# Seven products for eight in part of a SwiGLU FFN: two block pairs per layer by quadrants

## The chip, the cores and the metric

The kernel runs on one core of a Trainium2 chip. The metric is the device time of one execution in microseconds. TensorE (PE in the profile) multiplies matrices, VectorE (DVE) and ScalarE (ACT) do elementwise work, GpSimd (POOL) does small work for the norms, and SyncE (SP) issues the DMAs.

## The reference

Two layers of a hybrid encoder run over 256 tokens with a model width of 1024, in fp32. The part that is changed is the first half of the SwiGLU FFN and, by its place, the per-layer embedding:

```python
h = h + rms_norm(mixed @ w_out, g_mix_post)

gate, up = jnp.split(rms_norm(h, g_ffn_pre) @ w_ffn_in, 2, axis=-1)   # 1024 -> 2 * 2816
h = h + rms_norm((jax.nn.silu(gate) * up) @ w_ffn_out, g_ffn_post)

e = p_i @ w_ple_proj                                                  # 256 -> 1024
h = h + rms_norm(jax.nn.sigmoid(h @ w_ple_gate) * e, g_ple_post)
```

Ahead of it stand one projection of the normed state, two attention branches (gated linear attention and grouped-query attention) and their merge.

## The kernel before

**Numbers.** Every fp32 operand is split into a high part (a cast to the matmul's fp32r type, on ScalarE) and a low part (source minus high, on VectorE); this is `split`, lines 99 to 102, with the subtraction in `vsub` (line 97). A product takes three matmuls into one accumulator: high with high, high with low, low with high (`mm3`, line 87, recorded at line 85).

**Weights.** All weights pass through one `Stream` (line 177) in the order of the list `plan` (line 162). A unit is 128 partitions by 2048 fp32 values, 1 MB: four k-blocks of 128 rows by 512 columns. It is loaded by SyncE into one of two `raw` tiles, split in two halves of 1024 into one of four pairs of tiles `wh` and `wl`, and then used. `Stream.done` is called after the last matmul on a unit; it lets the next unit of the plan be split (`fill`), and once a raw tile has been split the next load is issued. At most `depth` units, four, are held split at a time.

**Tiles.** Tokens are worked in two halves of 128. `amode` (line 383) multiplies one half of the tokens (stationary, 128x128) by one unit (moving, 512 columns): 12 matmuls. `project` (line 417) does two units for both halves: 48 matmuls. Activations that are to be multiplied are transposed by TensorE and split into a `Split` (line 258), which has one large tile for the high parts and one for the low ones.

**Order around the change.** A `Task` is a piece of work that is put off: it waits for a number of ticks, and `tick` is called once for every six matmuls of a 128x512 product. So transposes are laid between matmuls of later work. `need` forces a task that is wanted at once. The framework puts every engine's instructions in an order of its own by priority, with all waits; `tc.high_priority` moves some ahead.

Per layer, the parts near the change run in this order:
- `wout`: `by_half` (line 426) first works the output projection for token half 0, then for half 1. After each half come `post_norm_add` and `pre_norm`, whose transposes into `u2` wait six ticks (`WAIT`).
- `emb`: the embedding's product, 24 matmuls on one unit, none of them with a tick. Its copies from the accumulators run on ScalarE (line 1023).
- `ffnin`: eleven blocks. A block is 256 gate columns and the same 256 up columns, so its two units hold gate and up side by side. For blocks 0 and 1 token half 0 goes first (48 matmuls), then half 1; blocks 2 to 10 go through `project`. Each block ends with a silu on ScalarE (lines 1038 and 1051) and a multiplication on VectorE (line 94); its transposes wait four ticks (`WAIT_FFN`).
- `ffnout`: eleven units of `w_ffn_out`, of which the last four are worked for half 0 first and then for half 1; then `post_norm_add` and the transposes of `h` into `hT`, five ticks later (`WAIT_H`).
- `ple`: the embedding's gate, by halves, with the embedding `e` as a factor.

The pools hold 2 `raw`, 4 `wh`, 4 `wl`, 9 `big` (2048 columns), 10 `mid` (1024), 5 `t512` and 8 accumulators (128x512).

Of the kernel before, what the change touches and what calls it, by code (L numbers as in the profile page):

```python
# [2 lines left out]

# [27 lines left out]
HIDDEN = 2816  # L31
NBLK = HIDDEN // 256
UNIT = 2112
RQ = ((0, 288), (288, 672), (672, 1056))
# [5 lines left out]
def trunk_kernel(ctx: ExitStack, tc: tile.TileContext, a: dict, out: bass.AP):  # L40
# [122 lines left out]
    for l in range(DEPTH):  # L163
        w = a["w_in"][l]
        plan += [unit_rows(w, n, C_RA, C_RA + 1056, 2 if l + n == 0 else 1) for n in range(4)]
        for c0 in (C_AK, C_GQ, C_GK, C_GV, C_GV + 512, C_GG, C_GG + 512, C_GA, C_GA + 512, C_GB, C_GB + 512):
            plan += [unit(w, kh, c0) for kh in range(2)]
        for j in range(2):
            for wo in (a["w_o_gla"][l], a["w_o_attn"][l]):
                plan += [unit(wo, kh, j * 512) for kh in range(2)]  # L170
        plan += [unit(a["w_out"][l], kh, j * 512) for kh in range(2) for j in range(2)]
        plan += [unit_rows(a["w_ple_proj"][l], 0)]
        plan += [unit_gate_up(a["w_ffn_in"][l], kh, b) for b in range(NBLK) for kh in range(2)]
        plan += [unit_rows(a["w_ffn_out"][l], n) for n in range(NBLK)]
        plan += [unit(a["w_ple_gate"][l], kh, j * 512) for kh in range(2) for j in range(2)]

    class Stream:


        def __init__(self, depth):  # L180
            self.depth, self.n, self.held, self.raws, self.ready, self.open = depth, 0, 0, [], [], False

        def load(self, between=lambda: None):

            if self.n == len(plan):
                return
            raw = rawp.tile([P, UNIT], F32, tag="raw", name=nm("raw"))
            moves = plan[self.n](raw)
            for dst, src in moves:
                if self.open:  # L190
                    nc.sync.dma_start(dst, src)
                else:
                    on("dma", nc.sync.dma_start, dst, src)
                between()
            self.raws.append((raw, sum(math.prod(dst.shape[1:]) for dst, _ in moves)))
            self.n += 1

        def pieces(self):

            raw, n = self.raws.pop(0)  # L200
# [4 lines left out]
            return [(wh[:, c], wl[:, c], raw[:, c]) for c in (slice(0, n // 2), slice(n // 2, n))]  # L205

        def fill(self):
            while self.open and self.held < self.depth and self.raws:
                for piece in self.pieces():
                    split(*piece)  # L210
                self.load()

# [4 lines left out]
        def done(self, n=1):  # L217
            self.held -= n
            self.fill()

# [37 lines left out]
    class Split:  # L258


        def __init__(self):
            self.h, self.l = (big(F32R).rearrange("p (k t) -> p k t", t=T) for _ in range(2))
            self.makers = {0: [], 1: []}

        def need(self, hf, k=None):
# [9 lines left out]
        def put(self, src, k, n, t0, tn):  # L275

            i = (slice(None), slice(k, k + n), slice(t0, t0 + tn))
            split(self.h[i], self.l[i], src.rearrange("p (k t) -> p k t", t=tn))

        def tok(self, k, hf):  # L280
            s = slice(hf * P, (hf + 1) * P)
            return self.h[:, k, s], self.l[:, k, s]

        def all(self, k):
            return self.h[:, k, :], self.l[:, k, :]

    def transpose_in(sp, src, k, n, hf):

        ps = aux()
        for i in range(n):  # L290
            nc.tensor.transpose(ps[:, i * P : (i + 1) * P], src[:, i * P : (i + 1) * P], ident)
        with tc.high_priority(AHEAD):
            sp.put(ps[:, : n * P], k, n, hf * P, P)

    last_pow = [None]
# [47 lines left out]

    def turn_in(sp, x, hf, wait):


        def turn():
            yield wait
            for j, y in enumerate(halves(x)):
                transpose_in(sp, y, 4 * j, 4, hf)  # L350

        sp.makers[hf].append(Task(turn(), part[0]))

    def pre_norm(g, hf, sp, wait=WAIT):

# [6 lines left out]

        turn_in(sp, xn, hf, wait)

# [27 lines left out]
    def wmode(os_, sp, k0, w, first, last):  # L392
# [9 lines left out]
        for f in range(4):  # L402
            o = os_[f // 2][:, (f % 2) * T : (f % 2 + 1) * T]
            s = slice(f * P, (f + 1) * P)
            for k in range(4):
# [3 lines left out]
                )  # L409
            tick()  # L410

    def project_t(sp):
# [113 lines left out]
    def turned(hf, k, n):  # L526

        ps = aux()
        for i in range(n):
            on("pe", nc.tensor.transpose, ps[:, i * P : (i + 1) * P], xn[hf][:, (k + i) * P : (k + i + 1) * P], ident)  # L530
        i = (slice(None), slice(k, k + n), slice(hf * P, (hf + 1) * P))
        split_here(uT.h[i], uT.l[i], ps[:, : n * P].rearrange("p (k t) -> p k t", t=P))

# [42 lines left out]
    for l in range(DEPTH):  # L576
# [413 lines left out]

        part[0] = f"{l}emb"
        e = big().rearrange("p (s c) -> p s c", s=2)
        pin = t512().rearrange("p (s c) -> p s c", c=256)
        nc.sync.dma_start(pin, a["p"][l, 0].rearrange("(s p) c -> p s c", p=P))
        pT = [t.rearrange("p (k t) -> p k t", t=T) for t in halves(mid(F32R))]
        ps = aux()
        for k in range(2):
            for hf in range(2):
                nc.tensor.transpose(
                    ps[:, k * T + hf * P : k * T + (hf + 1) * P], pin[:, hf, k * P : (k + 1) * P], ident  # L1000
                )
        split(pT[0], pT[1], ps.rearrange("p (k t) -> p k t", t=T))
# [4 lines left out]
        u2 = Split()  # L1007

        def after_out(hf, o):
            post_norm_add(o, gpost, hf)  # L1010
            pre_norm(gpre, hf, u2)

        by_half(mixT, after_out)

        part[0] = f"{l}emb"
        wh, wl = (t[:, :2048].rearrange("p (k c) -> p k c", c=512) for t in ws.take())
        for hf in range(2):
            s = slice(hf * P, (hf + 1) * P)
            for j in range(2):
                o = acc()  # L1020
                for k in range(2):
                    mm3(o, (pT[0][:, k, s], pT[1][:, k, s]), (wh[:, 2 * k + j, :], wl[:, 2 * k + j, :]), k == 0, k == 1)
                nc.scalar.copy(e[:, hf, j * 512 : (j + 1) * 512], o)
        ws.done()


        part[0] = f"{l}ffnin"
        hid = [Split() for _ in range(3)]
        us = [[ws.take() for _ in range(2)] for _ in range(2)]
        for hf in range(2):  # L1030
            for b in range(2):
                o = acc()
# [5 lines left out]
                nc.scalar.activation(sg[:, 0:256], o[:, 0:256], AF.Silu)  # L1038
                vmul(sg[:, 0:256], o[:, 256:512], sg[:, 0:256])


                def turn(sg=sg, b=b, hf=hf):
                    yield WAIT_FFN
                    transpose_in(hid[0], sg[:, 0:256], b * 2, 2, hf)

                hid[0].makers[hf].append(Task(turn(), part[0]))
        for b in range(2, NBLK):
            sg = t512()
            for hf, o in enumerate(project(u2)):
                c = slice(hf * 256, (hf + 1) * 256)  # L1050
                nc.scalar.activation(sg[:, c], o[:, 0:256], AF.Silu)
                vmul(sg[:, c], o[:, 256:512], sg[:, c])

            def turn(sg=sg, b=b):
                yield WAIT_FFN
                ps = aux()
                for k in range(2):
                    for hf in range(2):
                        nc.tensor.transpose(
                            ps[:, k * T + hf * P : k * T + (hf + 1) * P],  # L1060
                            sg[:, hf * 256 + k * P : hf * 256 + (k + 1) * P], ident,
                        )
                with tc.high_priority(AHEAD):
                    hid[b // 4].put(ps, 2 * b % 8, 2, 0, T)

            turned = Task(turn(), part[0], 2 * b % 8 // 4)
            for hf in range(2):
                hid[b // 4].makers[hf].append(turned)

        if l + 1 < DEPTH:  # L1070
            ropes = rope_tables(l + 1)
            wup_next = up_weights(l + 1)


# [5 lines left out]
        def out_step(n, hf, w):  # L1080
            wh, wl = (t[:, :2048].rearrange("p (k c) -> p k c", c=512) for t in w)
            for kk in range(2):
                k = 2 * n + kk
                hid[k // 8].need(hf, k % 8)
                for j in range(2):
                    mm3(
                        o[hf][j], hid[k // 8].tok(k % 8, hf), (wh[:, 2 * kk + j, :], wl[:, 2 * kk + j, :]),
                        k == 0, k == 2 * NBLK - 1,
# [10 lines left out]
        for hf in range(2):  # L1099
# [5 lines left out]

            turn_in(hT, h[:, hf, :], hf, WAIT_H)


# [77 lines left out]
```

## Time and profile before

| | us |
|---|---|
| median of 3 runs | 950.26 (949.28 to 950.45) |
| the profiled execution's own time | 950.44 |
| its span | 948.7 |
| TensorE busy in the span | 936.2 |
| VectorE busy | 612.8 |
| ScalarE busy | 509.9 |
| FFN-in of layer 0, start to end | 266.55 to 391.93 |

The profile is one execution with a record of every instruction. The page gives busy times, the chain of work that ended last and groups of instructions by line; the trace can also be asked for the time line of one engine, for the waits between engines, and for the busy time in any stretch. Matmul records overlap, because matmuls are pipelined: what one costs is seen from how far apart a run of them starts and ends. Where several instructions follow each other on an engine, the timeline merges them into one row with a count (x2).

### The profile page before, as it was taken

The numbers are of one execution on the slowest core, as the hardware profiler recorded it, in microseconds if no ns is written. First come the engines' busy times: TensorE is split into PE (matmuls) and PEld (weight loads), VectorE is DVE, ScalarE is ACT, GpSimd is POOL, SyncE is SP. The second block draws the span as 40 slices with busy tenths as digits, with TensorE's granted clock in tenths as the row PEclk, the third lists the DMA queues.
The fourth block names the chain that finished last, engine by engine and source line by source line (L and its number), as shares of the span: only waits on it lengthen the run. The fifth ranks groups of instructions, "written<-read, shape, count | busy, mean of one in ns | idle before, by whom it ended". The sixth has DMA issues, their size and how long they took to land.

```text
span 948.7 us, 12370 instructions
## 1 busy us (share of the span) xinstructions
PE 936.2 (99%) x4769; PEld 798.5 (84%) x4769; DVE 612.8 (65%) x838; ACT 509.9 (54%) x872; POOL 83.3 (9%) x152
## 2 busy tenths in 40 slices
PE   8999999999999999999999999999999999999996
PEld 7998888888888888888889988888888888888886
DVE  4798977456666555444779799663667665555364
ACT  4669776434465544443666686754436554443343
POOL 3400211000020000000133011200001000000010
PEclk9999999999999999999999999999999999999999
DMA  6463454655478655553545525355564666655531
GB/s 237 156 222 133 147 176 142 219 180 185 146 225 271 216 178 178 180 211 121 190 169 178 192 75 189 107 204 199 200 222 134 221 223 192 192 192 178 183 128 44
DMA packets 100760, 169.25 MB, mean 178 GB/s; under 512 B 3735, under 2 KB 51351, under 8 KB 100702
## 3 DMA queue, kind: packets, MB, share of 16 engines
q1 hardware_dynamic: 100702, 168.47, 52.7%
q8 instruction: 37, 0.61, 0.2%
q14 instruction: 21, 0.17, 0.0%
HBM read 167.41 MB, written 1.05 MB: 178 GB/s over the span
## 4 chain that ended last, share of the span: by engine, by line
PE 94%; DVE 2%; POOL 1%; ACT 1%; DMA 1%; issue 1%; SPq 0%; POOLq 0%; DVEq 0%; ACTq 0%
PE acc_0ffnin L85 13%; PE acc_1ffnin L85 13%; PE acc_0ffnout L85 6%; PE acc_1ffnout L85 6%; PE acc_0gate L85 5%; PE acc_1gate L85 5%; PE acc_1merge L85 5%; PE acc_0merge L85 5%; PE acc_1gqk L85 2%; PE acc_0rq L85 2%; PE acc_0gqk L85 2%; PE acc_1wout L85 2%; PE acc_0wout L85 2%; PE acc_1ple L85 2%; PE acc_1gg L85 2%; PE acc_0gg L85 2%
## 5 line engine op out<-in xcount | busy, mean ns | idle before, releaser
L85 PE MATMUL acc_0ffnin<-wh_0ffnin,big_0wout 128*128 128x512 f32 x288 | 91.3, 393 | 0.0
L85 PE MATMUL acc_1ffnin<-wh_1ffnin,big_1wout 128*128 128x512 f32 x288 | 91.3, 393 | 0.0
L97 DVE TENSOR_TENSOR wl_1ffnin<-raw_1ffnin,wh_1ffnin 128x1024 fp32r<-128x1024 f32 x40 | 47.9, 1221 | 48.4 <-ACT wh_1ffnin L101 48.4
L97 DVE TENSOR_TENSOR wl_0ffnin<-raw_0ffnin,wh_0ffnin 128x1024 fp32r<-128x1024 f32 x40 | 47.8, 1222 | 43.3 <-ACT wh_0ffnin L101 43.2
L101 ACT CAST wh_1ffnin<-raw_1ffnin 128x1024 fp32r<-128x1024 f32 x40 | 41.1, 1053 | 51.0 <-PE acc_1ffnin L85 38.2
L101 ACT CAST wh_0ffnin<-raw_0ffnin 128x1024 fp32r<-128x1024 f32 x40 | 40.8, 1052 | 44.7 <-PE acc_0ffnin L85 35.3
L85 PEld LDWEIGHTS acc_0ffnin<-wh_0ffnin,big_0wout 128*128 128x128 f32 x288 | 54.1, 188 | 11.0
L85 PEld LDWEIGHTS acc_1ffnin<-wh_1ffnin,big_1wout 128*128 128x128 f32 x288 | 54.1, 188 | 11.0
L85 PE MATMUL acc_1ffnin<-wl_1ffnin,big_1wout 128*128 128x512 f32 x144 | 56.1, 390 | 0.0
L85 PE MATMUL acc_0ffnin<-wl_0ffnin,big_0wout 128*128 128x512 f32 x144 | 56.1, 390 | 0.0
L85 PE MATMUL acc_0ffnout<-wh_0ffnout,big_0ffnin 128*128 128x512 f32 x112 | 34.9, 390 | 0.0
L85 PE MATMUL acc_1ffnout<-wh_1ffnout,big_1ffnin 128*128 128x512 f32 x112 | 34.9, 390 | 0.0
L97 DVE TENSOR_TENSOR wl_1ffnout<-raw_1ffnout,wh_1ffnout 128x1024 fp32r<-128x1024 f32 x18 | 21.3, 1222 | 18.4 <-ACT wh_1ffnout L101 18.4
L97 DVE TENSOR_TENSOR wl_0ffnout<-raw_0ffnout,wh_0ffnout 128x1024 fp32r<-128x1024 f32 x18 | 21.3, 1222 | 18.4 <-ACT wh_0ffnout L101 18.4
L85 PEld LDWEIGHTS acc_1ffnin<-wl_1ffnin,big_1wout 128*128 128x128 f32 x144 | 27.1, 188 | 5.3
L85 PEld LDWEIGHTS acc_0ffnin<-wl_0ffnin,big_0wout 128*128 128x128 f32 x144 | 27.1, 188 | 5.3
L101 ACT CAST wh_1ffnout<-raw_1ffnout 128x1024 fp32r<-128x1024 f32 x18 | 18.1, 1052 | 22.6 <-PE acc_1ffnout L85 22.6
L101 ACT CAST wh_0ffnout<-raw_0ffnout 128x1024 fp32r<-128x1024 f32 x18 | 18.2, 1053 | 22.5 <-PE acc_0ffnout L85 19.8
L97 DVE TENSOR_TENSOR wl_1gate<-raw_1gate,wh_1gate 128x1024 fp32r<-128x1024 f32 x14 | 16.5, 1222 | 17.8 <-ACT wh_1gate L101 17.8
L97 DVE TENSOR_TENSOR wl_0gate<-raw_0gate,wh_0gate 128x1024 fp32r<-128x1024 f32 x14 | 16.5, 1222 | 17.8 <-ACT wh_0gate L101 17.8
L85 PE MATMUL acc_0rq<-wh_start,big_start 128*128 128x384 f32 (+1 forms) x96 | 25.4, 349 | 0.9 <-ACT big_start L111 0.9
L85 PE MATMUL acc_0gate<-wh_0gate,big_start 128*128 128x512 f32 x80 | 24.8, 389 | 0.0
(587 smaller groups left out, 2672.7 us busy)
## 6 DMA issues: line engine op xcount, KB each, us to landing
raw_0ffnin<-in_w_ffn_in_dram SPq DMA_DIRECT2D x32, 512.0 KB, 4.2
raw_1ffnin<-in_w_ffn_in_dram SPq DMA_DIRECT2D x32, 512.0 KB, 3.9
raw_0ffnin<-in_w_ffn_out_dram SPq DMA_DIRECT2D x6, 1024.0 KB, 5.0
raw_1ffnin<-in_w_ffn_out_dram SPq DMA_DIRECT2D x6, 1024.0 KB, 4.9
raw_0ffnout<-in_w_ffn_out_dram SPq DMA_DIRECT2D x5, 1024.0 KB, 4.9
raw_1ffnout<-in_w_ffn_out_dram SPq DMA_DIRECT2D x5, 1024.0 KB, 4.9
raw_0rq<-in_w_in_dram SPq DMA_DIRECT2D x4, 1024.0 KB, 5.0
raw_0v<-in_w_in_dram SPq DMA_DIRECT2D x4, 1024.0 KB, 4.8
```

What stands on the lines that cost most here:

```text
L85: return nc.tensor.matmul(o, lhsT, rhs, start=start, stop=stop)
L97: nc.vector.tensor_tensor(out=out, in0=in0, in1=in1, op=ALU.subtract)
L101: nc.scalar.copy(hi, src)
```

## The change

Blocks 2 and 3, and blocks 6 and 7, are worked as pairs. A pair is a product of the 256x1024 normed activations with 1024x1024 weights (512 gate columns and 512 up columns). Both are cut into quadrants: token half by half of the 1024 rows, and half of the rows by gate or up. The four quadrant results are made from seven products of 12 matmuls with sums of quadrants (the scheme of Winograd) in place of eight. The four activation sums are made once per layer on VectorE, from fp32 copies of the transposed activations (`plain`, copied by ScalarE), and split (`sums`). The weight sums are made on VectorE for each pair, in place, in the tiles that the raw quadrants were loaded into (`Stream.step`): two quadrants are loaded into a `wh` and a `wl` tile that the stream lends, which counts as one held unit; one goes into a `big` tile and one into a `raw` tile. After each of the first, second, third and fifth splits an addition of 128x2048 prepares a later one. The results of the products are combined by copies on ScalarE and additions on VectorE (`seven`), and two accumulators stay open over much of the pair.

`FFN_IN` gives the order after blocks 0 and 1: u is one unit of a plain block (both token halves, 24 matmuls), a digit is that product of a pair. The plain blocks are 4, 5, 8, 9 and 10. The transposes of a pair's hidden columns wait nine ticks.

The embedding moves: its load of `p`, the transposes and the split stand behind FFN-in, its weights' unit is loaded behind `w_ffn_out`, and its product stands between `ffnout` and `ple`. `Split` now has one tile for four k-blocks, with high and low parts side by side, taken when first written.

```diff
+FFN_IN = "uu12u34u5u67uu12u34u5u67"
+WAIT_PAIR = 9
+PLAIN, PAIRS = (4, 5, 8, 9, 10), (2, 6)
...
-        plan += [unit_rows(a["w_ple_proj"][l], 0)]
-        plan += [unit_gate_up(a["w_ffn_in"][l], kh, b) for b in range(NBLK) for kh in range(2)]
-        plan += [unit_rows(a["w_ffn_out"][l], n) for n in range(NBLK)]
+        w = a["w_ffn_in"][l]
+        blocks = [[unit_gate_up(w, kh, b) for kh in range(2)] for b in range(NBLK)]
+        plan += blocks[0] + blocks[1]
+        plains = [u for b in PLAIN for u in blocks[b]]
+        pairs = [[unit(w, kh, c + b * 256) for kh in range(2) for c in (0, HIDDEN)] for b in PAIRS]
+        for x in FFN_IN:
+            if x == "1":
+                pair = pairs.pop(0)
+            plan.append(plains.pop(0) if x == "u" else (pair, int(x)))
+        plan += [unit_rows(a["w_ffn_out"][l], n) for n in range(NBLK)]
+        plan += [unit_rows(a["w_ple_proj"][l], 0)]
...
+                    if n == 1:
+                        b11, b12, b21, b22 = units
+                        x, z = (Load(b, lambda tag=tag: self.lent(tag), tag == "wh") for b, tag in ((b11, "wh"), (b12, "wl")))
+                        y, q = Load(b22, big), Load(b21)
+                        self.loads += [x, y, z]
+                    if n == 5:
+                        self.loads.append(q)
...
+        def lent(self, tag):
+            if tag == "wh":
+                self.held += 1
+                self.lend = False
+            return wp.tile([P, UNIT], F32R, tag=tag, name=nm("lent")).bitcast(F32)
...
+        def start(self, between=lambda: None):
+            while self.loads and (self.lend or not self.loads[0].waits) and (self.loads[0].own or self.room):
...
+        def step(self, n, x, y, z, q):
+            c = slice(0, 2048)
+            if n == 1:
+                self.made(x)
+                nc.vector.tensor_tensor(out=x.raw[:, c], in0=x.raw[:, c], in1=z.raw[:, c], op=ALU.add)
+            elif n == 2:
+                self.made(y)
+                nc.vector.tensor_tensor(out=z.raw[:, c], in0=z.raw[:, c], in1=y.raw[:, c], op=ALU.add)
+            elif n == 3:
+                self.made(x)
+                nc.vector.tensor_tensor(out=x.raw[:, c], in0=x.raw[:, c], in1=y.raw[:, c], op=ALU.add)
+            elif n == 4:
+                self.made(z)
+            elif n == 5:
+                self.made(x)
+                nc.vector.tensor_tensor(out=x.raw[:, c], in0=x.raw[:, c], in1=q.raw[:, c], op=ALU.add)
+            elif n == 6:
+                self.made(q)
+            else:
+                self.load()
+                self.made(x)
+                self.held -= 1
+                self.lend = True
...
+            (a11, a12), (a21, a22) = x
+            s2 = t512()
+            vsub(a22, a21, a22)
+            vsub(s2, a11, a22)
+            vsub(a12, a12, s2)
+            yield 1
+            vsub(a21, a21, a11)
+            for s in (a12, a22, a21, s2):
+                parts = halves(mid(F32R))
+                split(*parts, s)
...
+        (p1, v), (p3, p7), (c12, c22) = (halves(mid()) for _ in range(3))
+        c11 = acc()
+        times(c11, quad(0, 0))
+        nc.scalar.copy(p1, c11)
+        yield
+        task.need()
+        o = acc()
+        times(o, form(0))
+        nc.scalar.copy(p3, o)
+        yield
+        p5 = acc()
+        times(p5, form(1))
+        yield
+        o = acc()
+        times(o, form(2))
+        nc.scalar.copy(p7, o)
+        yield
+        o = acc()
+        times(o, form(3))
+        vsub(v, o, p1)
+        add(v, p5, v)
+        add(c12, v, p3)
+        add(c22, v, p7)
+        yield
+        times(c11, quad(0, 1), False)
+        gated(0, c11, c12)
+        yield
+        times(p5, quad(1, 1), False)
+        vsub(v, p5, c22)
+        gated(1, v, c22)
+        yield
...
         for hf in range(2):
+            ws.lend = hf == 1
...
+                if (hf, b) == (1, 0):
+                    forms = sums(plain)
...
+        steps, pairs, seven_ = chain.from_iterable(block(b) for b in PLAIN), list(PAIRS), None
+        for x in FFN_IN:
+            if x == "1":
+                seven_ = pair(pairs.pop(0))
+            next(steps if x == "u" else seven_)
+        ws.lend = False
```

More of the change, by code (lines that the diff above doesn't have):

```diff
@@ L2 @@
 from contextlib import ExitStack, nullcontext
+from itertools import chain
 import concourse.bass as bass
@@ L201, in pieces, with put @@
+        def put(self, x, parts=2):
             wh = wp.tile([P, UNIT], F32R, tag="wh", name=nm("wh"))
@@ L218, in done @@
             self.held -= n
+            self.start()
             self.fill()
@@ L293, in transpose_in @@
             sp.put(ps[:, : n * P], k, n, hf * P, P)
+        if plain is not None:
+            nc.scalar.copy(plain, ps[:, : n * P])
     last_pow = [None]
@@ L342, in halves, with turn_in @@
         return [t[:, j * 512 : (j + 1) * 512] for j in range(2)]
-    def turn_in(sp, x, hf, wait):
+    def turn_in(sp, x, hf, wait, plain=None):
         def turn():
@@ L410, in wmode, with times, sums, make @@
             tick()
+    def times(o, act, first=True):
+        wh, wl = (t[:, :2048].rearrange("p (k c) -> p k c", c=512) for t in ws.take())
+        for k in range(4):
+            (ah, al), h, lo = act(k), wh[:, k, :], wl[:, k, :]
+            for n, (x, y) in enumerate(((ah, h), (ah, lo), (al, h))):
+                nc.tensor.matmul(
+                    o, x, y, start=first and k + n == 0, stop=k == 3 and n == 2, skip_group_check=not first
+                )
+            if k % 2:
+                tick()
+        ws.done()
+    def sums(x):
+        made = []
+        def make():
+            yield 1
[4 more added lines that the diff above has]
+            vsub(a12, a12, s2)
+            yield 1
+            vsub(a21, a21, a11)
+            for s in (a12, a22, a21, s2):
+                parts = halves(mid(F32R))
+                split(*parts, s)
+                made.append([p.rearrange("p (k t) -> p k t", t=P) for p in parts])
+                yield 1
+        return made, Task(make(), part[0])
+    def seven(sp, forms, gated):
+        made, task = forms
+        quad = lambda hf, j: lambda k: sp.tok(4 * j + k, hf)
+        form = lambda i: lambda k: [p[:, k, :] for p in made[i]]
+        def add(out, x, y):
+            nc.vector.tensor_tensor(out=out, in0=x, in1=y, op=ALU.add)
+        (p1, v), (p3, p7), (c12, c22) = (halves(mid()) for _ in range(3))
[29 more added lines that the diff above has]
+        yield
     def project_t(sp):
```

214 lines of the change are left out of this document (133 added, 81 removed).

## The prediction

> **What bounds the kernel now.** I read the page's engine table first, then the chain that ended last, then the waits of TensorE (the third fence).
>
> ```profile
> span 948.7 us, 12370 instructions
> ...
> PE 936.2 (99%) x4769; PEld 798.5 (84%) x4769; DVE 612.8 (65%) x838; ACT 509.9 (54%) x872; POOL 83.3 (9%) x152
> ```
> ```profile
> PE 94%; DVE 2%; POOL 1%; ACT 1%; DMA 1%; issue 1%; SPq 0%; POOLq 0%; DVEq 0%; ACTq 0%
> ```
> ```profile
> PE aux_0ple L291 <- DVE mid_0ple L339: 1.7, 2, 1.4
> PE warm L111 <- POOL ident masks.py:199: 1.5, 1, 1.5
> PE acc_0rq L85 <- ACT big_start L111: 0.9, 1, 0.9
> PE acc_0kv L85 <- DVE wl_0rq L97: 0.4, 1, 0.4
> PE acc_1rq L85 <- DVE wl_0ple L97: 0.3, 1, 0.3
> PE aux_start L111 <- DVE mid_start L111: 0.2, 1, 0.2
> ```
>
> TensorE is busy for 936.2 of 948.7 us and makes up 94% of the chain. Its longest waits are at the layer boundary and at the start; no line names ffnin. So time is saved only by taking matmuls out, as long as nobody makes TensorE wait afterwards. The question is what one matmul is worth and how much room VectorE has. The next view is the chain, in order of time, around FFN-in of layer 0; then the busy time by stage.
>
> ```profile
> 254.82 2.52 PE acc_0wout L85 x11
> 257.34 0.87 PE aux_0wout L291 x8
> 258.21 2.88 PE acc_0wout L85 x24
> 261.09 5.47 PE acc_0emb L85 x24
> 266.55 8.17 PE acc_0ffnin L85 x36
> 274.72 0.87 PE aux_0wout L291 x8
> 275.59 2.75 PE acc_0ffnin L85 x12
> 278.35 0.22 PE aux_0ffnin L291 x2
> 278.56 5.48 PE acc_0ffnin L85 x24
> 284.04 0.22 PE aux_0ffnin L291 x2
> 284.26 5.46 PE acc_0ffnin L85 x24
> ...
> 306.97 10.93 PE acc_0ffnin L85 x48
> ```
> ```profile
> core 0: us, PE busy (x) PEld busy (x) DVE busy (x) ACT busy (x) POOL busy (x), PEclk, DMA share, GB/s
> ...
> 289.00:391.00 102.00, 102.00 (x469) 84.43 (x468) 57.82 (x67) 49.40 (x67) 0.00 (x0) 1.00 0.64 208
> ```
> ```profile
> L85 PE MATMUL acc_0ffnin<-wh_0ffnin,big_0wout 128*128 128x512 f32 x288 | 91.3, 393 | 0.0
> ```
>
> The group's mean of 393 ns is not what a matmul costs: matmuls overlap. 24 of them end 5.46 us after they began (284.26), so one is worth 227.5 ns, at a clock of 1.00. In the nine blocks from 289 to 391 TensorE is full, VectorE is busy for 57.82 of 102 us and ScalarE for 49.40.
>
> **The saving.** A plain unit is 24 matmuls (two halves of the tokens, four k, three terms), 5.46 us. A pair of blocks is four units, 96 matmuls. As seven products of 12 it is 84. Two pairs in each of two layers save 4 x 12 = 48 matmuls, and 48 x 0.2275 = 10.9 us. The transposes stay the same in number, and the embedding's 24 matmuls (5.47 us) only move. [...]
>
> **VectorE, the price.** A product lasts 2.73 us on TensorE, but its weights need a split like those of a plain unit, and four of seven jobs also an add of 128x2048. The rows for these:
>
> ```profile
> L97 DVE TENSOR_TENSOR wl_0ffnin<-raw_0ffnin,wh_0ffnin 128x1024 fp32r<-128x1024 f32 x40 | 47.8, 1222 | 43.3 <-ACT wh_0ffnin L101 43.2
> ...
> L101 ACT CAST wh_0ffnin<-raw_0ffnin 128x1024 fp32r<-128x1024 f32 x40 | 40.8, 1052 | 44.7 <-PE acc_0ffnin L85 35.3 <-DMA raw_0ffnin<-in_w_ffn_in_dram 9.4
> ```
> ```profile
> L94 DVE TENSOR_TENSOR t_0ffnin<-acc_0ffnin,t_0ffnin 128x256 f32<-128x256 f32 x22 | 9.2, 420 | 2.9 <-ACT t_0ffnin L1038 2.8
> ...
> L982 DVE TENSOR_TENSOR big_0gate<-big_0gate,big_0gate 128x512 f32<-128x512 f32 x4 | 2.8, 692 | 0.1
> ```
> ```profile
> 330.37 1.23 DVE L97 TENSOR_TENSOR wl_0ffnin<-raw_0ffnin,wh_0ffnin 128x1024 fp32r<-128x1024 f32 x1 [2.74 <-ACT wh_0ffnin L101]
> 331.51 0.68 DVE L97 TENSOR_TENSOR big_0ffnin<-aux_0ffnin,big_0ffnin 128x512 fp32r<-128x512 f32 x1
> 332.11 1.22 DVE L97 TENSOR_TENSOR wl_0ffnin<-raw_0ffnin,wh_0ffnin 128x1024 fp32r<-128x1024 f32 x1
> 333.24 0.42 DVE L94 TENSOR_TENSOR t_0ffnin<-acc_0ffnin,t_0ffnin 128x256 f32<-128x256 f32 x1
> ```
>
> The last view is VectorE's timeline: in a queue the next instruction starts 1.14 us behind a 1.23 us one and 0.60 behind a 0.68 one. No row has 128x2048. From 692 ns (512) to 1222 ns (1024) an element costs 1.035 ns, so the add is 1222 + 1060 = 2.28 us, 2.2 start to start; above it bound by two of 1222 ns, 2.44, below by two at 1.14.
>
> Per layer, with full durations: six more units are split (28 for 22), 12 x 1.22 = 14.7 us; eight adds, 18.3; the activations' sums, four subtractions and four splits of 128x512, 8 x 0.69 = 5.5; two times five additions on product sums, 6.9; four products with silu of 512 columns for eight of 256, -0.6. That is 44.8 on top of 57.8, 102.6 us, while TensorE's stretch shrinks to 102 - 5.5 = 96.5. Start to start (1.14, 2.2, 0.60, and 0.34 for 256 columns, 0.42 less the same overlap) the nine blocks, each with four splits, two products and one transposed split, are 9 x 5.84 = 52.6 and the additions 41.7, together 94. So VectorE goes from 57% to between 97% and 106% of the stretch. Exposed time per layer: between 0 and 102.6 - 96.5 = 6.1 us. A gain from this is excluded: nothing is taken off VectorE that TensorE waited for.
>
> Where in this range depends on the queue. While a pair runs, one slot is lent to its sums, and three instead of four are left: when token i ends, token i+3 is split, and the cover is tokens i+1 and i+2. I walk the order uu12u34u5u67 with start-to-start costs, in us from the start of the second token half of blocks 0 and 1. Behind u0, u1, the sums and job 1, VectorE finishes job 2's split at 24.4 (product 2 begins at 25.0), its add at 26.6, the third u's first half at 27.7 (begins 28.2), job 3 with its add at 34.6, job 4's first half at 35.8 (begins 36.4), the fourth u's at 38.0 (begins 39.1), job 5 by 43.6. From there it gains room: job 7 ends at 51.2, wanted at 55.9. So the densest stretch has 0.5 to 1 us of slack after 28 us of queued work, and 3% more per instruction, a cast that comes late, or one add put ahead of a split use it up. Full durations are 7% more; that would be late by some 1.5 us per pair. I take 1 us per pair, nearer to the start-to-start rows since a full queue is what those show: 4 us in all, ends 0 and 12.2.
>
> [...]
>
> ScalarE: 12 more casts (12.6 us), four copies of u, three of products per pair, four casts of sums; under 70 of 96 us, covered. DMA: the same bytes at a share of 0.64; a pair's three loads go out together, 3 x 1.05 MB (about 10 us at 208 GB/s / 0.64), issued 8 us before job 1 and wanted from then to job 1's add, another 8 us: just covered. SP's queue waits there for the lent slot, and the next plain unit's load stands behind it; it is wanted 14 us later.
>
> **The embedding moves.** At ffnout's end it only adds cover: that place shows no wait of TensorE. At FFN-in's start its 5.47 us covered the second half's norm. The rows of that chain:
>
> ```profile
> 265.87 0.63 ACT L324 ACTIVATE t_0wout<-h 128x512 f32<-128x512 f32 x1
> ...
> 266.50 0.57 ACT L1023 COPY big_0emb<-acc_0emb 128x512 f32<-128x512 f32 x1
> ...
> 274.77 1.28 ACT L1038 ACT_TABLE_LOAD   x1
> 276.06 0.39 ACT L1038 ACTIVATE t_0ffnin<-acc_0ffnin 128x256 f32<-128x256 f32 x1
> ```
> ```profile
> 268.77 1.41 DVE L339 SCALAR_TENSOR_TENSOR mid_0wout<-h,rstd_0wout,mid_0wout 128x512 f32<-128x512 f32 x2 [1.36 <-POOL rstd_0wout L335]
> 270.10 2.35 DVE L97 TENSOR_TENSOR wl_0wout<-raw_0wout,wh_0wout 128x1024 fp32r<-128x1024 f32 x2
> ```
>
> The normed half is ready at 270.18, 9.1 us after wout's end at 261.09. Its transposes came at 274.72, 13.6 us after; now they come six ticks after the end, at 8.2. So they wait 0.9 us, less the embedding's copy (0.57) that stood between the squares, or more if the silu's table load and first silu (1.67), now ready earlier, go in front: 0 to 2.6. The fourth unit is split where the third was (270.10); its first half is there at 271.2, wanted at 270.2, and the two waits overlap. 1 us per layer, 2 in all, ends 0 and 5.2.
>
> Sum: 950.44 (span 948.7 and 1.74 around it) - 10.9 + 4 + 2 = 945.5. The profiled execution lies 0.18 above the median of the runs, 950.26, so I leave it there.
>
> **The rivals.** (1) The whole saving arrives: VectorE keeps its half microsecond everywhere and the norm's chain shortens, 950.44 - 10.9 = 939.5. For it: the start-to-start walk never misses. Against: at 97% nothing is left for a single late cast. (2) VectorE is the bound by full durations, with 6.1 us per layer exposed: -10.9 + 12.2, and with part of the lost cover about 951, no change. For it: 102.6 against 96.5; against: the 1.14 us starts, and backlog may run into ffnout, where VectorE has room. (3) Slower: the adds, 16 in the kernel, stand in VectorE's queue ahead of the split that TensorE waits for next. Each that is wholly exposed costs 2.2 us, so above 10.9 / 16 = 0.68 us per add, less than a third of it, the change loses. With half of each exposed, 17.6 us plus 2 at the boundary: 950.44 - 10.9 + 19.6 = 959. For it: adds are issued right behind their job's split, ahead of later jobs in an in-order engine. Against: the walk has them there already and still meets each start.
>
> **How the numbers follow.** My forecast, with costs between 2.5 and 9 us, has 0.53; rival 1 0.20; rival 2 0.12; rival 3 0.15. The measurement can tell about 0.2%, 1.9 us. The forecast and rival 1 are faster, as is a quarter of rival 2: 0.76; the rest of rival 2 is the same: 0.09; rival 3 slower: 0.15. The range is from 939.0, the full saving less half a microsecond of spread between runs (949.28 to 950.45), to 950.5, nearly no change, where the costs reach 11; it leaves out rival 3 and the upper part of rival 2.
>
> **What would show it.** Matmuls of ffnin per layer 24 fewer; blocks of 12 matmuls in 2.73 us; VectorE's busy share above 0.9 in FFN-in with most of its idle time before the low parts gone; TensorE waiting on VectorE for low parts in ffnin, near the third and fourth u of each order, 1 us per pair; a wait of the u2 transposes on the scaled norm under 1 us at FFN-in's start; no wait at ple. The forecast is wrong if TensorE waits over 9 us in ffnin, if it waits on the DMA of a lent slot or for an accumulator that a product holds, or if 12 matmuls take other than 2.73 us.

## The result and the profile after

The changed kernel takes 942.36 us, the median of 4 runs (941.98 to 942.66), against 950.36 (949.28 to 950.56) for the kernel before: a ratio of 0.9918, with an interval from 0.9901 to 0.9935. A repeat on another chip (e12) gave 943.01 and a ratio of 0.9924. The saving is 8.0 us; 4.9 had been forecast (945.5).

The same lines of the page after as were shown of the page before:

```profile
span 940.9 us, 12357 instructions
...
PE 927.7 (99%) x4721; PEld 788.9 (84%) x4721; DVE 695.6 (74%) x906; ACT 547.0 (58%) x916; POOL 90.2 (10%) x152
...
PE 85%; DVE 6%; DMA 3%; ACT 2%; POOL 2%; issue 2%; SPq 0%; POOLq 0%; DVEq 0%; ACTq 0%
```

There are 48 matmuls fewer, and TensorE is busy 8.5 us less. VectorE has 82.8 us more work, and its part of the chain has gone from 2% to 6%, DMA's from 1% to 3%. TensorE still has 99%. The waits of TensorE in the kernel after (engine, line and operation that waited, what it waited for: total us, times, longest us):

```profile
PE aux_0ple L397 <- DVE mid_0ple L447: 1.6, 2, 1.4
PE warm L116 <- POOL ident masks.py:199: 1.5, 1, 1.5
...
PE acc_1ffnin L527 <- DVE mid_1ffnin L566: 0.2, 1, 0.2
PE acc_1ffnin L90 <- DVE wl_1wout L102: 0.2, 1, 0.2
PE acc_0ffnin L90 <- DVE wl_0wout L102: 0.2, 1, 0.2
```

FFN-in now has names here, but each with 0.2 us. L527 is a product of a pair. L566 is `add` in `seven`, an addition on VectorE that combines the products' results: the seventh product goes on adding to an accumulator that this addition must have read first. The sums of activations (`sums`) are named in no wait. The chain of FFN-in in layer 0 (start, us, what) shows how near VectorE is:

```profile
267.38 1.15 DVE wl_0wout L102
268.57 2.80 PE acc_0ffnin L90 x11
271.36 0.22 PE aux_0ffnin L397 x2
271.58 5.49 PE acc_0ffnin L90 x24
...
296.94 2.35 DVE wl_0ffnin L102 x2
299.29 0.34 DVE t_0ffnin L99
299.68 0.33 PE aux_0ffnin L1238
...
311.26 5.44 PE acc_0ffnin L90 x24
316.70 2.72 PE acc_0ffnin L527 x12
319.43 2.72 PE acc_0ffnin L90 x12
```

A product of 12 matmuls takes 2.72 us. From 277 to 299.7 the chain runs through VectorE's queue and ScalarE, up to the product of silu and up (L99) that a plain block's transposes (L1238) wait for; then TensorE has it again. For 23 us VectorE sets the pace and TensorE is only just not waiting. VectorE's idle time ahead of the low parts has gone, from 43.3 us in this group in the kernel before to 3.2 (layer 0):

```profile
L102 DVE TENSOR_TENSOR wl_0ffnin<-raw_0ffnin,wh_0ffnin 128x1024 fp32r<-128x1024 f32 x28 | 33.2, 1226 | 3.2 <-ACT wh_0ffnin L106 3.1
```

The busy time by stage in the kernel after (start:end, length, then busy us and count of PE, PEld, DVE, ACT and POOL, the granted clock, DMA's share and rate):

```profile
core 0: us, PE busy (x) PEld busy (x) DVE busy (x) ACT busy (x) POOL busy (x), PEclk, DMA share, GB/s
282.00:379.50 97.50, 97.30 (x443) 79.72 (x442) 93.41 (x94) 61.82 (x81) 4.63 (x3) 1.00 0.53 178
480.64:484.05 3.41, 1.64 (x11) 1.11 (x10) 2.75 (x4) 3.38 (x5) 0.57 (x1) 1.00 0.03 9
484.05:487.47 3.42, 3.42 (x13) 3.42 (x14) 2.20 (x3) 0.49 (x2) 0.00 (x0) 0.50 0.38 84
```

In the nine blocks VectorE is busy for 93.41 of 97.5 us (96%), TensorE for 97.30. The last two rows lie at the boundary between the layers: TensorE idles half of the first and gets half of its clock in the second.

Cut by stages at TensorE's first matmul of kv, wout and ple in each layer, in us (FFN is wout to ple and holds the embedding):

| kernel | start to kv | kv to wout | FFN 0 | ple to kv | kv to wout | FFN 1 | rest |
|---|---|---|---|---|---|---|---|
| before | 38.5 | 198.4 | 216.1 | 51.7 | 197.6 | 216.0 | 30.5 |
| after | 36.9 | 197.7 | 212.6 | 52.9 | 197.2 | 213.1 | 30.5 |
| difference | -1.6 | -0.7 | -3.5 | +1.3 | -0.3 | -3.0 | 0 |

The four transposes of `p` (0.11 us each, 0.44 in each layer) moved with the embedding from the second and fifth column into FFN. Put back, the FFN stages gain 3.9 and 3.4 us and the columns they left nearly nothing. The -1.6 and the +1.3 are the clock's, see the last section.

### The profile page after: what moved, and what is told of

Same layout as the page of the kernel before. It is cut to its first block, busy times and chain, and to the rows that moved or that the text cites. A ratio compares the mean times of both kernels' runs of the same rounds, so it can differ in the third digit from the quotient of the medians.

```text
span 940.9 us, 12357 instructions
## 1 busy us (share of the span) xinstructions
PE 927.7 (99%) x4721; PEld 788.9 (84%) x4721; DVE 695.6 (74%) x906; ACT 547.0 (58%) x916; POOL 90.2 (10%) x152
## 4 chain that ended last, share of the span: by engine, by line
PE 85%; DVE 6%; DMA 3%; ACT 2%; POOL 2%; issue 2%; SPq 0%; POOLq 0%; DVEq 0%; ACTq 0%
PE acc_1ffnout L90 6%; PE acc_0ffnout L90 6%; PE acc_1ffnin L90 6%; PE acc_0ffnin L90 6%; PE acc_0gate L90 5%; PE acc_1gate L90 5%; PE acc_1merge L90 5%; PE acc_0merge L90 5%; PE acc_0ffnin L527 4%; PE acc_1ffnin L527 3%; PE acc_1gqk L90 2%; PE acc_0gqk L90 2%; PE acc_1ple L90 2%; PE acc_1gg L90 2%; PE acc_0gg L90 2%; PE acc_1v L90 2%
## 5 line engine op out<-in xcount | busy, mean ns | idle before, releaser
L90 PE MATMUL acc_1ffnin<-wh_1ffnin,big_1wout 128*128 128x512 f32 x160 | 51.8, 394 | 0.0
L90 PE MATMUL acc_0ffnin<-wh_0ffnin,big_0wout 128*128 128x512 f32 x160 | 51.8, 394 | 0.0
L102 DVE TENSOR_TENSOR wl_1ffnin<-raw_1ffnin,wh_1ffnin 128x1024 fp32r<-128x1024 f32 x28 | 32.9, 1218 | 5.1 <-ACT wh_1ffnin L106 5.1
L102 DVE TENSOR_TENSOR wl_0ffnin<-raw_0ffnin,wh_0ffnin 128x1024 fp32r<-128x1024 f32 x28 | 33.2, 1226 | 3.2 <-ACT wh_0ffnin L106 3.1
L90 PEld LDWEIGHTS acc_0ffnin<-wh_0ffnin,big_0wout 128*128 128x128 f32 x160 | 30.0, 188 | 6.1
L90 PEld LDWEIGHTS acc_1ffnin<-wh_1ffnin,big_1wout 128*128 128x128 f32 x160 | 30.0, 188 | 6.1
L90 PE MATMUL acc_0ffnin<-wl_0ffnin,big_0wout 128*128 128x512 f32 x80 | 31.2, 390 | 0.0
L90 PE MATMUL acc_1ffnin<-wl_1ffnin,big_1wout 128*128 128x512 f32 x80 | 31.2, 390 | 0.0
L90 PE MATMUL acc_1gate<-wh_1gate,big_0ple 128*128 128x512 f32 x80 | 24.8, 389 | 0.0
L90 PEld LDWEIGHTS acc_0ffnout<-wh_0ffnout,big_0ffnin 128*128 128x128 f32 x112 | 21.0, 188 | 4.4
```

What stands on the lines that cost most here:

```text
L90: return nc.tensor.matmul(o, lhsT, rhs, start=start, stop=stop)
L102: nc.vector.tensor_tensor(out=out, in0=in0, in1=in1, op=ALU.subtract)
```

## The experiments

**Theory A**, the prediction's: the seven products bring the 10.9 us, VectorE takes a few of them back because it is just not full enough to be the bound, and the embedding's move costs a little. **Rival B** differed from run to run: the gain comes from the layout or the embedding's move, or VectorE has nothing to do with what is lost.

**e1: the layout alone.** The kernel before with the new `Split`.

```diff
-            self.h, self.l = (big(F32R).rearrange("p (k t) -> p k t", t=T) for _ in range(2))
+            self.t = {}
...
+                self.t[k // 4] = big(F32R).rearrange("p (k s t) -> p k s t", s=2, t=T)
```

> The kernel before, with the new layout of the transposed activations alone (one tile for four k-blocks, high and low parts side by side, taken when first written). Theory A (the 8 us come from FFN-in; the 1.9 us by which the changed kernel was ahead at the first layer's keys come and go with the moment at which TensorE's clock rises, not with the code): 950.3, within 1 us of before. Rival B (the layout lets the start go faster, so that the full clock comes at 13.0 instead of 16.3 us): about 948.4, and full clock from about 13 us in its trace.

Measured 950.09 (11 runs), ratio 0.9999 (0.9990 to 1.0008). The layout does nothing.

**e2: the embedding's move alone.** The kernel before with the embedding where the change puts it.

```diff
-        plan += [unit_rows(a["w_ple_proj"][l], 0)]
...
         plan += [unit_rows(a["w_ffn_out"][l], n) for n in range(NBLK)]
+        plan += [unit_rows(a["w_ple_proj"][l], 0)]
```

> The kernel before, with the embedding's load, transposes and product moved behind FFN-out alone; no seven products. Theory A (the move takes the cover away at FFN-in's start, where the changed kernel's trace has 0.7 us of waits per layer, and gives nothing back): 951.7, 0.5 to 2 us slower than before. Rival B (the move is worth something by itself, through cover at FFN-out's end): 949 or less.

Measured 951.21 (11 runs), ratio 1.0017 (1.0006 to 1.0027). The waits of TensorE in e2 have the row that was expected for the fourth unit's low part:

```profile
PE acc_0ffnin L85 <- DVE wl_0wout L97: 0.2, 1, 0.2
PE acc_1ffnin L85 <- DVE wl_1wout L97: 0.2, 1, 0.2
```

The FFN stages grow by 1.8 and 0.9 us, 0.44 of each the moved transposes: 1.4 and 0.4 for the lost cover. So A holds: the move by itself costs 1 to 2 us, and the gain is not from it.

**e3: the pairs with the embedding early.** The kernel after with the plan's item, the load, the transposes and the product back in their places of before.

```diff
+        plan += [unit_rows(a["w_ple_proj"][l], 0)]
         w = a["w_ffn_in"][l]
...
-        plan += [unit_rows(a["w_ple_proj"][l], 0)]
```

> The changed kernel, with the embedding back at its old place ahead of FFN-in (its weights' unit too). Theory A: the waits at FFN-in's start (0.7 us per layer) go and nothing else changes: 941.0. Rival B (the move carries part of the gain): 944 or more.

Measured 942.71 (5 runs), ratio 0.9923 (0.9910 to 0.9936): neither, no difference from the kernel after. The waits of TensorE in e3 say why:

```profile
PE acc_1ffnin L527 <- DVE mid_1ffnin L566: 0.6, 1, 0.6
PE acc_0ffnin L527 <- DVE mid_0ffnin L566: 0.6, 1, 0.6
```

The row of FFN-in's start is gone, and the first pair's seventh product waits 0.6 us instead, for the addition that must have read its accumulator. Against the full saving the FFN stages lose 3.5 us in both layers together, where the kernel after loses 3.6. With pairs, the place of the embedding here only chooses which of two waits stands in FFN-in.

**e4 and e5: the adds, none and twice.** The kernel after without the four adds in `Stream.step`, and with each written twice.

```diff
-                nc.vector.tensor_tensor(out=x.raw[:, c], in0=x.raw[:, c], in1=z.raw[:, c], op=ALU.add)
...
```

> The changed kernel without the four additions of weight quadrants per pair (16 in all, 2.28 us each on VectorE); the products then run on unsummed quadrants. Theory A (the queue hides nearly all of VectorE's work, as the trace's waits of TensorE in FFN-in, about 0.6 us per layer, say): 941.2, 0.5 to 1.5 us less than the changed kernel. Rival B (the adds cost 1 us per pair or more, as the prediction took, in stretches that the waits do not show): 938.5 or less.

> The changed kernel with each of the four weight additions per pair made twice (the sums then hold a quadrant twice). Per layer VectorE's list grows by 8 x 2.2 = 17.6 us, start to start, from 94 to about 112 in a stretch of 96.5 us of TensorE. Theory A (VectorE is hidden now only because its list just fits; past the stretch every us counts, less 3 to 5 us per layer that the queue can give back in FFN-out): 965, 960 to 973. Rival B (VectorE has real room, the 97% of the prediction's list was counted too high): 946 or less.

Without adds: 940.65 (4 runs), ratio 0.9902 (0.9889 to 0.9916). Twice: 968.18 (4 runs), ratio 1.0182 (1.0165 to 1.0199). Both as A had it. In e4's nine blocks VectorE falls to 77.09 of 97.5 us busy and the FFN stages to 212.4 and 212.0: they gain 0.2 and 1.1 us, so 16 adds of 2.28 us, 36.5 us of work, cost TensorE 1.3 us there. Only the sum of the layers carries this: in the repeat of the kernel after (e12) the same stages take 213.0 and 212.5, which would make it 0.6 and 0.5. Another 1.3 us of the two profiles' difference of 2.1 is the slow stretch at the boundary, which e4's trace lacks, and its start is 0.4 longer. The next 36.5 us of adds cost 25.8 us.

VectorE's row of one such add in the kernel after, and the nine blocks in e4, busy time by stage as above:

```profile
L285 DVE TENSOR_TENSOR lent_0ffnin<-lent_0ffnin,big_0ffnin 128x2048 f32<-128x2048 f32 x2 | 4.6, 2281 | 0.0
```
```profile
282.00:379.50 97.50, 97.50 (x445) 80.57 (x444) 77.09 (x88) 62.98 (x82) 4.33 (x2) 1.00 0.54 180
```

The waits of TensorE in e5 (L1242 is a transposition of a plain block's hidden columns):

```profile
PE aux_1ffnin L1242 <- DVE t_1ffnin L99: 7.2, 3, 4.5
PE aux_0ffnin L1242 <- DVE t_0ffnin L99: 7.0, 3, 4.5
```

And the busy time by stage in e5, columns as above:

```profile
301.27:304.68 3.41, 0.06 (x1) 0.00 (x0) 3.41 (x3) 0.85 (x2) 0.00 (x0) 1.00 0.00 0
304.68:308.09 3.41, 2.23 (x7) 1.88 (x8) 3.41 (x5) 2.31 (x3) 0.00 (x0) 0.50 0.41 106
308.09:311.51 3.42, 3.42 (x9) 2.64 (x8) 3.42 (x4) 0.00 (x0) 0.00 (x0) 0.50 1.05 405
311.51:314.92 3.41, 3.41 (x16) 2.78 (x15) 3.41 (x3) 0.18 (x1) 0.00 (x0) 1.00 0.29 107
```

TensorE stands at the transposes of a plain block's hidden columns. They are laid into its stream by ticks and need a product on VectorE (L99) that stands behind the adds. The matmuls behind them wait too: in the first row TensorE is busy for 0.06 of 3.41 us, while VectorE has no gap (3.41). Then TensorE has half of its clock for 6.83 us, and later in each layer once more for 3.41: 10.2 us per layer, in which about 5 us of work are lost (in the rows above, 9 matmuls in 3.42 us at half clock and 16 in 3.41 at full). The FFN stages grow by 13.7 and 12.9 us: about 5 the clock, the rest waits.

**e6: the same work, without plain units between the products.**

```diff
-FFN_IN = "uu12u34u5u67uu12u34u5u67"
+FFN_IN = "uuuuu1234567uuuuu1234567"
```

> The changed kernel with the order uuuuu1234567, twice, in place of uu12u34u5u67: the same work on every engine, but a pair's seven products stand in a row. Theory A (what hides VectorE is that plain units of 5.46 us stand between products of 2.73, since only two tokens of cover stand ahead of a split): 2 to 4 us lost per pair, 952, 948 to 958. Rival B (only the sums over the stretch matter): 942.5, as the changed kernel.

Measured 954.94 (4 runs), ratio 1.0042 (1.0027 to 1.0057): A. The waits of TensorE in e6 stand right behind the pairs: in the plain unit behind the first, and at the start of FFN-out behind the second:

```profile
PE acc_0ffnin L90 <- DVE wl_0ffnin L102: 1.4, 1, 1.4
...
PE acc_0ffnout L90 <- DVE wl_0ffnin L102: 0.9, 1, 0.9
...
PE acc_0ffnin L90 <- ACT wh_0ffnin L106: 0.5, 1, 0.5
```

VectorE's work is the same, but within a row of products there are 2.72 us of matmuls to each split and add, with no plain unit between to make up for it. VectorE falls behind (from 311 to 330 us it is busy for 18.0 of 19.0), and the unit behind the pair waits for its split. About 4 us of waits per layer, and 3.41 us of half clock behind the longest of them. Laying the products apart is worth 12 us, more than the whole gain.

**e7 and e8: one pair per layer, and three.**

```diff
-FFN_IN = "uu12u34u5u67uu12u34u5u67"
+FFN_IN = "uu12u34u5u67uuuuuuuuu"
-PLAIN, PAIRS = (4, 5, 8, 9, 10), (2, 6)
+PLAIN, PAIRS = (4, 5, 6, 7, 8, 9, 10), (2,)
```

and for three:

```diff
+FFN_IN = "u12u34567u12u34567u12u34567"
+PLAIN, PAIRS = (6, 7, 10), (2, 4, 8)
```

> The changed kernel with one pair per layer (blocks 2 and 3) and seven plain blocks. Theory A (each pair is worth 2.73 us, and the waits at FFN-in's start, 1.5 us in all, stay): 950.2 - 5.5 + 1.5 + 0.4 = 946.6. Rival B (the first pair carries the fixed cost of the activation sums, and the second is nearly free): 948 or more.

> The changed kernel with three pairs per layer (blocks 2, 4 and 8 begin one) and three plain blocks, in the order u12u34567, three times. TensorE has 16.4 us less than before in all; VectorE's list per layer is about 113 us start to start against a stretch of 93.8 of TensorE. Theory A (VectorE becomes the bound, with 4 to 6 us per layer of it given back in FFN-out): 942.4 - 5.5 + 2 x 14 = 965, 957 to 973. Rival B (TensorE stays the bound): 938.

One pair: 950.71 (10 runs), ratio 1.0004 (0.9994 to 1.0014). Three: 981.62 (4 runs), ratio 1.0334 (1.0317 to 1.0351). A has the direction of three and not the size, and its size for one is wrong: half the matmuls saved give none of the time. B's number for one pair fits. The waits of TensorE in e7:

```profile
PE aux_0ffnin L1238 <- DVE t_0ffnin L99: 1.4, 1, 1.4
...
PE acc_1ffnin L527 <- DVE mid_1ffnin L566: 0.8, 1, 0.8
PE acc_0ffnin L527 <- DVE mid_0ffnin L566: 0.5, 1, 0.5
```

Where two of these stand in layer 0 (timelines of VectorE and of TensorE in e7: start, us, what):

```profile
328.99 0.69 DVE L566 TENSOR_TENSOR mid_0ffnin<-acc_0ffnin,mid_0ffnin 128x512 f32<-128x512 f32 x1
```
```profile
329.82 0.47 PE L527 MATMUL acc_0ffnin<-wh_0ffnin,big_0wout 128*128 128x512 f32 x1 [0.45 <-DVE mid_0ffnin L566]
...
368.85 0.33 PE L1238 MATMUL aux_0ffnin<-ident,t_0ffnin 128*128 128x128 f32 x1 [1.40 <-DVE t_0ffnin L99]
```

TensorE loses 3.4 us in FFN-in of layer 0 and 1.9 in layer 1, by the starts of its matmuls; with two pairs it loses 1.2 and 1.5. The boundary at FFN-in's start is 1.0 and 0.7 of it. The pair's seventh product, which waits until L566 has read its accumulator, is 0.6 and 1.0, counted by the starts. A transposition that waits for an L99 product is 0.2 in each layer, and another, at 368.85, 1.6 in layer 0. No wait names the activation sums, which B had as the cause; their subtractions and splits stand in VectorE's queue in the first pair's stretch, and how much of the first pair's waits is theirs is not shown. From the first pair to the wait at 368.85 the chain of e7 runs through the loads, round after round like these:

```profile
320.37 5.16 DMA raw_0ffnin<-in_w_ffn_in_dram
...
325.63 1.06 ACT wh_0ffnin L106
...
326.72 2.37 DVE wl_0ffnin L102 x2
...
329.51 4.98 DMA raw_0ffnin<-in_w_ffn_in_dram
```

Each load waits for a raw tile that the split before it frees. Load, cast and split of one tile take 9.1 us, so two tiles bring a unit every 4.6 us, and a plain unit lasts 5.46: what a pair has delayed is made up by less than 1 us per unit, and in e7 nothing but plain units follows. So the costs do not count per pair: the boundary is paid once per layer; with two pairs all but 0.2 us of the waits behind it stand at the first pair; and in e7's layer 0 the units that follow the pair run into loads. e7's FFN stages (217.8 and 216.1) lose 4.0 and 2.3 us against their own saving of 2.7 with the transposes' 0.44 put back; 0.6 and 0.4 of these I cannot place. With three pairs the order has 21 products among six plain units, and TensorE waits about 15 us per layer (in layer 0, 6.6 on L99 products, 4.4 and 1.7 on low parts among them) and has 10.2 us of half clock per layer, as in e5.

**e9: the adds on GpSimd.**

```diff
-                nc.vector.tensor_tensor(out=x.raw[:, c], in0=x.raw[:, c], in1=z.raw[:, c], op=ALU.add)
+                nc.gpsimd.tensor_tensor(out=x.raw[:, c], in0=x.raw[:, c], in1=z.raw[:, c], op=ALU.add)
...
```

> The changed kernel with the four weight additions per pair on GpSimd, which the changed kernel's trace shows idle in most of FFN-in. Theory A (GpSimd and VectorE get in each other's way: the changed kernel's trace has GpSimd's 128x256 products at 2.14 us in FFN-in beside a busy VectorE, 0.74 us in the kernel before beside a less busy one, so an add of 128x2048 takes 6 to 17 us, and the third and later splits come late): 955 or more. Rival B (the adds leave VectorE's queue, and the time is that of the kernel without them): 941.

Measured 974.57 (4 runs), ratio 1.0263 (1.0246 to 1.0279). Groups of e9 (line, engine, operation, shapes, count | busy us, mean ns | idle before):

```profile
L285 POOL TENSOR_TENSOR lent_0ffnin<-lent_0ffnin,big_0ffnin 128x2048 f32<-128x2048 f32 x2 | 10.3, 5147 | 0.2
...
L102 DVE TENSOR_TENSOR wl_0ffnin<-lent_0ffnin,wh_0ffnin 128x1024 fp32r<-128x1024 f32 x20 | 31.5, 1616 | 1.9 <-ACT wh_0ffnin L106 1.9
...
L102 DVE TENSOR_TENSOR wl_1ffnin<-big_1ffnin,wh_1ffnin 128x1024 fp32r<-128x1024 f32 x4 | 17.8, 4466 | 0.0
```

The first of these VectorE groups in the kernel after:

```profile
L102 DVE TENSOR_TENSOR wl_0ffnin<-lent_0ffnin,wh_0ffnin 128x1024 fp32r<-128x1024 f32 x20 | 23.5, 1218 | 0.4 <-ACT wh_0ffnin L106 0.3
```

A's time holds, its cause in part. An add took 4.6 to 5.1 us where A said 6 to 17, but VectorE's splits beside it took longer too, 1616 and 4466 ns where they take 1218 and 1217 in the kernel after. TensorE then stands at the same transposes for up to 7.5 us. So moving 36.5 us off VectorE frees nothing: its busy time in the whole kernel rises from 695.6 to 712.9 us. On VectorE an add took 2.28 us; why the splits take longer beside GpSimd's adds is not shown.

**e11: three plain units before the first pair, the second right behind.**

```diff
-FFN_IN = "uu12u34u5u67uu12u34u5u67"
+FFN_IN = "uuu12u34u5u67u12u34u5u67"
```

> The changed kernel with one more plain unit ahead of the first pair and one less between the pairs: uuu12u34u5u67u12u34u5u67. Theory A (the 0.3 us per layer that product 2 waits for the activation sums go, and the second pair's lent load, wanted one unit earlier, still lands in time): 941.8. Rival B (the second pair's load or VectorE's queue is late): 944 or more.

Measured 948.38 (12 runs), ratio 0.9987 (0.9977 to 0.9997): B, by the second pair's load. The rows at L566, which A wanted gone, are gone from TensorE's waits, but they were the seventh product's and not the second's. The timelines of SyncE and of ScalarE in e11 (start, us, what):

```profile
331.78 0.92 SPq L252 DMA_DIRECT2D lent_0ffnin<-in_w_ffn_in_dram  x2
...
340.81 2.00 ACT L106 CAST wh_0ffnin<-lent_0ffnin 128x1024 fp32r<-128x1024 f32 x2 [1.80 <-DMA lent_0ffnin<-in_w_ffn_in_dram]
```

A pair's loads can go out only when the slot that the first pair was lent is free, and then take 8.6 us. With one unit between the pairs instead of two, ScalarE waits 1.80 us for them, and in layer 0 the second pair's second and third product wait 0.9 us each, the plain unit beside them 0.4 and a transposition behind them 1.0. The two plain units between the pairs are cover for a transfer.

**e12: the kernel after again**, for its time on another chip and for the clock.

> The changed kernel once more, beside the same runs of before. Theory A (the moment at which TensorE's clock becomes full differs from run to run and not from kernel to kernel): 942.4 again, and its trace may show the full clock anywhere between 12.9 and 16.3 us, and half clock near 484 us or not. Rival B: full clock from 13.0 us again and half clock at 484.

Measured 943.01 (5 runs, 940.76 to 943.24), ratio 0.9924 (0.9910 to 0.9937). Its two rows at the boundary, busy time by stage as above:

```profile
481.93:485.35 3.42, 1.66 (x11) 1.23 (x11) 2.87 (x4) 3.39 (x5) 0.51 (x1) 1.00 0.01 3
485.35:488.76 3.41, 3.41 (x14) 3.41 (x14) 2.07 (x3) 0.36 (x1) 0.00 (x0) 0.50 0.40 102
```

The half clock at the boundary is there again; the full clock at the start comes at 14.31 us and not at 13.01. So A on the start, B on the boundary.

## Why the prediction was right, point by point

- **The saving, -10.9.** Right: 48 matmuls fewer, 12 in 2.72 us (2.73 forecast).
- **VectorE's work.** Right: the prediction put its list at 94 us in 96.5; it is busy 93.41 of 97.5. The adds take 2.28 us, as interpolated. The rows of the kernel before carried this term well: split, product and start-to-start time were all measured there.
- **VectorE exposed, +4.** Too large. By the starts of TensorE's matmuls it is 0.5 and 0.8 us per layer, 1.3 in all: 0.26 us twice in layer 0, at 299.68 and 328.18, and three of 0.2 to 0.4 in layer 1. In e12, the same kernel, it is 0.7 in all. The prediction had 1 us per pair; the walk itself had found no miss, and I added for late casts; none shows in TensorE's waits here. The place was off too: it named the low parts of the third and fourth u; what waits first is a transposition for the product at L99, in the kernel after by 0.26 us and in e5 by 4.5. The second to wait, at 328.18 and in layer 1 for 0.4 us, is the first pair's seventh product, until VectorE has read its accumulator. That is one of the signs by which the prediction said it would be wrong, a wait for an accumulator that a product holds: it did show, with 0.6 us in all.
- **FFN-in's start, +2.** 0.7 us per layer, 1.4 in all; in e12 1.3 and 0.7, the 2 that was forecast. The two waits that it named are there, in the other proportion: the scaled norm 0.14 us, the fourth unit's low part 0.43 and 0.11 (the chain's 267.38 and 268.57). In e2, by itself, it is 1.4 and 0.4 us.
- **No wait at ple** from the move: right, 1.6 us there as in before (1.7).
- **What the sum lacked.** The FFN stages lose 1.6 and 2.1 us against their full saving; the two terms above explain 2.7 of these 3.6. The rest, 0.9, I cannot place. So -10.9 + 3.6 = -7.3; with -0.1 in the other stages and the clock's -1.6 and +1.3, which the prediction did not price, this is -7.7, and the span's difference is -7.8. The clock's two shares nearly cancel in this pair of profiles, by chance. As far as these two show, the saving beyond the forecast comes from the smaller exposure and not from the clock.
- **Rival 1**, nothing exposed, 939.5: not reached, but the kernel ends nearer to it than the forecast's middle. **Rival 2**, VectorE as the bound: wrong for the kernel after. (Its sum was off as well: 950.44 - 10.9 + 12.2 is 951.7 before any lost cover, not about 951.) VectorE does become the bound when its list grows: 36.5 us more cost 25.8. **Rival 3**, adds ahead of what TensorE needs: the mechanism is real, with an L99 product in the place of the split (e5). Its price per add here is 1.3 / 16, under 0.1 us, where it had to be 0.68.

No kernel that ran is faster than the changed one: e3 is equal, and e4 leaves work out.

## What to carry to other kernels

Trading matmuls for elementwise sums pays as long as the engine that makes them has room within the very stretch, and here it fits by 4 us in 97.5: the same work in a denser order (e6) or 18 us more per layer (e5) loses more than the change gains, and a shorter gap for a load (e11) loses most of it. So walk the second engine's queue in order with start-to-start times before building, with the transposes and what they need in it, and the accumulators that its additions must read before they can be used again, and not the weights' splits alone. Do not scale the result by halves or to three: one pair gave nothing, two gave 8 us, three lost 31.

## What the runs showed of the hardware

**The half clock.** In the record of the granted clock, the slow stretch at the boundary begins at 484.05 us in the kernel after, at 485.35 in e12 and at 486.66 in e3: each time 471.04 us after the first full clock of the same profile (13.01, 14.31 and 15.62). Behind the first full clock, each stretch of half clock in the 13 profiles lasted 3.41 or 6.83 us, apart from those at the kernels' ends. TensorE's busy time in rows of 3.41 us, cut from the first full clock on (138 rows in 471.04 us): half clock followed rows with 0.06 us (e5), 1.59 (e6), 1.64 (the kernel after), 1.65 (e8), 1.66 (e12) and 1.72 (e3); it did not follow rows with 1.73 (e12), 1.97 (e7), 2.07 (e4) and 2.36 (the kernel before), nor, at the kernels' ends, with 1.61 (e9) and 1.65 (e7). So in these profiles it was not the length of an idle stretch alone that went with half clock, but also how much of it fell into one such row. The kernel before, at the same boundary, busy time by stage:

```profile
483.87:487.29 3.42, 2.69 (x17) 2.37 (x15) 1.48 (x3) 2.72 (x6) 1.07 (x5) 1.00 0.78 287
487.29:490.70 3.41, 2.36 (x16) 1.94 (x16) 3.41 (x4) 3.04 (x4) 0.00 (x0) 1.00 0.00 0
```

The idle 1.8 us are cut into 0.7 and 1.1 there, and the clock stays full; in the kernel after 1.77 fall into one row (that of 480.64 above), 1.64 us of work in it did not keep the clock full, and the stage is 1.3 us longer.

**The full clock at the start** came between 12.96 and 16.26 us in the 13 profiles, 16.26 in e1 and 12.96 in e2, and at 13.01 and 14.31 in two profiles of the same kernel. From 14 to 16 us, 8 matmuls run in the kernel before and 14 in the kernel after. It moves a profile by up to 1.7 us (the first stage of the table takes 38.5 us in the kernel before, with 16.25, and 36.8 in e2): in one profile that is as much as a term of the sum, and only the medians and the stage table tell them apart.
